# Attention in pairs of heads: 512-column value products, the output copied in the middle of a unit, and the adaLN sums moved by one unit

## The chip, the cores and the metric

The kernel is one program on one NeuronCore of a Trainium2 chip. The metric is the device time of one execution in microseconds. The kernel before takes 2616.31 us (median of 3 runs, 2615.91 to 2618.69).

Names used below: PE is TensorE (PEld its weight loads), DVE is VectorE, ACT is ScalarE, POOL is GpSimd, SP is the engine that issues most DMAs. "L988" is line 988 of the kernel before.

## What is computed

The reference is a two-layer encoder trunk on 1024 positions of width 1024, all in float32. Layer 0 mixes tokens by grouped-query softmax attention (16 query heads of 64, 4 key/value heads), layer 1 by a chunked gMLP; each is followed by a squared-ReLU MLP, and every sub-layer is modulated by vectors that come from the conditioning vector `c` (adaLN).

```python
for i in range(DEPTH):
    mod = cond @ ada_w[i] + ada_b[i]
    sh1, sc1, g1, sh2, sc2, g2 = jnp.split(mod, N_MOD, axis=-1)
    h = modulate(rmsnorm(x, norm1_g[i]), sh1, sc1)
    y = gqa_attention(...) if i % 2 == 0 else chunked_gmlp(...)
    x = x + g1[:, None, :] * y
    h = modulate(rmsnorm(x, norm2_g[i]), sh2, sc2)
    x = x + g2[:, None, :] * sq_relu_mlp(h, mlp_w_in[i], mlp_w_out[i])
...
def one_block(q_blk):
    s = jnp.einsum('bqkgd,bskd->bkgqs', q_blk, k).astype(jnp.float32) * scale
    p = jax.nn.softmax(s, axis=-1).astype(v.dtype)
    return jnp.einsum('bkgqs,bskd->bqkgd', p, v)
```

The change touches mostly the attention of layer 0.

## The kernel before

**Precision.** The fast matmul format of the kernel is fp32r. To keep float32 accuracy most operands are split into a rounded part `hi` (a copy on ACT, a CAST in the profile) and the rest `lo = x - hi` (a subtraction on DVE), and a product takes two or three matmuls: hi*hi, hi*lo, lo*hi.

**Attention, by units.** A unit is one head and a quarter of the queries: 256 queries, as two blocks of 128 (`j` = 0, 1). There are 64 units: 4 quarters (`qq`) by 4 key/value groups (`g`) by 4 heads (`h4`). Each unit goes through stages:

- s (L947, matmuls at L952): scores of one query block with all 1024 keys, 4 matmuls of 512 columns into a two-bank PSUM tile (`ps_s`, 2 tiles); then DVE takes the negated row maximum (L955).
- e (L958): ACT's exponential of the 1024 scores with the maximum as bias, row sums as a by-product (L961), from PSUM to an SBUF tile `p_`. It frees the score tile.
- t (L965): 4 PE transposes (L969) bring two 128-key chunks of both query blocks into one PSUM bank; ACT copies the bank to `hi` (L972).
- h (L975): DVE makes `lo` (L978), which frees the bank.
- v (L981): the value product. The values of a group lie as 128 stationary columns, 64 of their hi part and 64 of their lo part; a chunk of 128 keys is 2 matmuls (hi and lo of the probabilities) of 256 columns each (L988), 16 per unit, summed into `u.po`, half a PSUM bank. After the last, ACT copies the two 64-row halves of `po` out (L998, L1000).
- f (L1003): POOL adds the two halves (L1005), 64 x 256.

Transposed chunks and `po` share four PSUM banks (`p_x`, handed out by `bank_x`) with the query transposes (q) and small sums.

**The order is written out by hand.** `ORDER` lists the stages of one loop iteration; a letter, then the age of the unit it works on (0: this iteration's, 1: the one before, 2: two before), then the piece. `pin` keeps these instructions in this order on each engine's queue; instructions that are not pinned are placed by the scheduler when they are ready. An engine's queue runs in order, so an instruction that waits holds all behind it.

```python
ORDER = "s00 v20 t10 q10 h10 t11 e00 s01 h11 t12 h12 v21 t13 e01 h13 v22 v23 q00 f20 m00"
```

`q00` prepares queries on POOL every fourth iteration (`q_stage`, L679, unpinned), `q10` transposes them on PE and copies them on ACT in two of four (`q_trans`, L934). `m00` is the place for side work:

- iterations 2 to 13: squares, sums, reciprocal roots and rotary positions of the queries of the second half of the sequence (`late_sums`, `late_rope`, `late_rope1`);
- adaLN columns on DVE (`mod_ahead`, L218): a 512 KB load in every fourth iteration from 15 to 51, and in a later one a multiply with sum over 128x1024 (L225) and a 128x1 add (L226), ten times; in the kernel before this comes at the end of iterations i with i % 4 == 1;
- adaLN sums on POOL (`Slabs.step`, L186): a 128x1024 multiply (L197 or L199) and a 128x1024 add (L200), 24 steps from iteration 14 on, in iterations with i % 4 of 1 or 2 or i % 8 == 3;
- from iteration 53 on (`WO_AT`): normalising the finished first half for the output projection (`wo_sums`, `wo_prep`).

**Memory.** Tiles of 128x512 come from a pool "t" of 58 buffers (`slot`), of 128x1024 from small pools "w", "s" and "c". The probabilities `p_` lie in "c" (4 buffers). All later phases (the MLPs and gMLP, in Strassen-Winograd form with `split` forms of activations, and `Out`, the second products) share these pools.

Of the kernel before, what the change touches and what calls it, by code (L numbers as in the profile page):

```python
# [18 lines left out]
P = 128  # L19
# [17 lines left out]
def encoder_kernel(ctx: ExitStack, tc: tile.TileContext, t: dict, out: bass.AP):  # L37
# [22 lines left out]
    def slot(dt=F32, shape=(P, 512)):  # L60
        return mem.tile(list(shape), dt, tag="t", name=nm("t"), bufs=SLOTS["t"])

# [300 lines left out]
    def forms_b(f, xt, layer, which, rb, order, apart=False):  # L363
# [10 lines left out]
        def forms(kt):  # L374
# [8 lines left out]
            f[("6", kt)] = split(t2)  # L383
# [11 lines left out]
        def later(q):  # L395
            for kt in range(4):
                f[(q, kt)] = split(src[q][kt])
                src[q][kt] = None
# [149 lines left out]
    if True:  # L548
# [7 lines left out]
        def qkv_hi(cb, kp, keep):  # L556
            raw = wide("c", F32, (2, CB))
            nc.sync.dma_start(raw, t["wqkv"][cb, kp])
            for i in range(2):
                if not keep:  # L560
                    hi, lo = slot(F32R), slot(F32R)
# [78 lines left out]
        def qk_rope(src, i, tt, nt=1, eng=V, add=None):  # L640
# [4 lines left out]
            dst, t2 = slot(), slot()  # L645
            xv, tv = heads(src, nt), heads(t2, nt)
            hold(eng.tensor_tensor(heads(dst, nt), xv, tab(0, 0, HD), ALU.mult))
            for a, b in ((0, 32), (32, 0)):
                hold(eng.tensor_tensor(tv[:, :, :, a : a + 32], xv[:, :, :, b : b + 32], tab(1, a, 32), ALU.mult))
            hold((add or eng).tensor_tensor(dst, dst, t2, ALU.add))  # L650
            return dst

        def qk_rstd(ss):
            ms = ss.rearrange("p a b -> p (a b)")
            hold(V.tensor_scalar(ms, ms, 1.0 / HD, EPS, ALU.mult, ALU.add))
            return rsqrt_small(ms, ms.shape[1])

        def q_sums(src):
            return qk_rstd(qk_sums(src))
# [11 lines left out]
        def k_rows(hf, src):  # L671
            return [qk_rope(src[j], 1, hf * 4 + 2 * j, 2) for j in range(2)]
# [199 lines left out]
        qkv_mm(2, 1, ps, hs1)  # L872
# [33 lines left out]
    def wo_prep(hf, dt):  # L906
# [4 lines left out]
        hi, lo = slot(F32R), slot(F32R)  # L911
# [20 lines left out]
    with ExitStack() as es:  # L932
# [13 lines left out]

        def s_stage(u, j):  # L947
# [10 lines left out]
        def e_stage(u, j):  # L958
            ps, mx = u.s[j]
            p_ = wide("c")  # L960
            pin(S.activation(p_, ps, AF.Exp, bias=mx,  # L961
                             accum_out=rowsum[:, 2 * u.qq + j, u.head : u.head + 1]))
            u.p.append(p_)

        def t_stage(u, sp):  # L965
            pt = bank_x("t")
            for s in range(2):
                for j in range(2):
                    pin(T.transpose(pt[:, (2 * s + j) * P : (2 * s + j + 1) * P],  # L969
                                    u.p[j][:, (2 * sp + s) * P : (2 * sp + s + 1) * P], ident))  # L970
            hi = slot(F32R)
            pin(S.copy(hi, pt))  # L972
            u.t.append((pt, hi))

        def h_stage(u, sp):  # L975
            pt, hi = u.t[sp]
            lo = slot(F32R)
            pin(V.tensor_tensor(lo, pt, f32(hi), ALU.subtract))  # L978
            u.pt.append((hi, lo))

        def v_stage(u, sp):  # L981
            if sp == 0:
                u.po = bank_x("o", (P, 256))
            hi, lo = u.pt[sp]
            for s in range(2):
                st = 2 * sp + s
                for part, src in ((0, hi), (1, lo)):
                    pin(T.matmul(u.po, vt[st][:, u.g * P : (u.g + 1) * P], src[:, s * 256 : (s + 1) * 256],  # L988
                                 start=st == 0 and part == 0, stop=st == 7 and part == 1))
            if sp < 3:  # L990
                return
            dt, hf = u.head // 2, u.qq // 2
            if (dt, hf) not in ot:
                ot[(dt, hf)] = slot()
            a = (u.head % 2) * 64
            b = 64 - a
            dst = ot[(dt, hf)][a : a + 64, (u.qq % 2) * 256 : (u.qq % 2) * 256 + 256]
            pin(S.copy(dst, u.po[b : b + 64]))  # L998
            src = slot()[a : a + 64, :256]
            pin(S.copy(src, u.po[a : a + 64]))  # L1000
            u.fin = (dst, src)

        def f_stage(u, _):  # L1003
            dst, src = u.fin
            pin(G.tensor_tensor(dst, src, dst, ALU.add))  # L1005

        stages = dict(s=s_stage, e=e_stage, t=t_stage, h=h_stage, v=v_stage, f=f_stage)
        units = []
        for qq in range(4):
            for g in range(NKV):  # L1010
                for h4 in range(4):
                    u = Unit()
                    u.qq, u.g, u.h4, u.head = qq, g, h4, 4 * g + h4
                    u.s, u.p, u.t, u.pt = [], [], [], []
# [7 lines left out]
        qkv_mm(2, 2, ps, hs1)  # L1022
        units[0].qst = nxt
        s_stage(units[0], 0)
        e_stage(units[0], 0)
        qkv_mm(2, 3, ps, hs1, (0,))
        s_stage(units[0], 1)
        e_stage(units[0], 1)
        qkv_mm(2, 3, ps, hs1, (1,))
# [4 lines left out]
        def late_sums(j):  # L1034
            rr2[j] = q_sums(r2[j : j + 1])
# [16 lines left out]
        for i in range(nu + 2):  # L1052
            u0 = units[i] if i < nu else None
            u1 = units[i - 1] if 0 < i <= nu else None
            u2 = units[i - 2] if i > 1 else None
# [4 lines left out]
            for op in ORDER.split():  # L1060
                f, w, j = op[0], int(op[1]), int(op[2])
                if f == "m":
# [13 lines left out]
                    if late_mods and i % 4 == 1:  # L1076
# [9 lines left out]
                else:  # L1086
                    u = (u0, u1, u2)[w]
                    if u and (i or f not in "se"):
                        stages[f](u, j)
# [11 lines left out]
    class Out:  # L1101
# [73 lines left out]
        def split_f(self, k):  # L1175
            self.f[k] = split(self.raw.pop(k))
# [592 lines left out]
SLOTS = {"t": 58, "x": 16, "w": 4, "s": 5}  # L1769
# [100 lines left out]
```

## Time and profile before

| | us |
|---|---|
| median of 3 runs | 2616.31 |
| profiled execution | 2620.57 |
| its span, first to last instruction | 2618.8 |
| busy: PE / DVE / ACT / POOL | 2593.0 / 2179.8 / 1443.7 / 718.5 |
| attention units: first s to last v matmul begin | 153.0 to 548.5 |
| mean granted clock of PE | 0.998 |

The profile is of one execution. "Busy" of an engine is the time in which at least one of its instructions ran. PE's instructions overlap: a matmul's duration holds its latency, so what it costs in a stream is read from the distance between the starts of neighbours. The same holds, more weakly, of ACT and DVE: a CAST that is shown as 0.59 us lets the next begin after 0.48 us. In the views of instructions in time, a row is one instruction or a run of equal ones: its start, its length, engine, line, operation, tiles and count.

### The profile page before, as it was taken

To read this page: it belongs to the slowest core of one execution; us is meant where nothing else is said; L and a number is where in the kernel's file an instruction comes from. 1 tells how busy PE (TensorE), PEld (TensorE's weight loads), DVE (VectorE), ACT (ScalarE), POOL (GpSimd) and SP (SyncE) were. 2 spreads that over 40 slices of the span, in tenths; PEclk is the share of its full clock that TensorE was granted. 3 is DMA by queue.
4 is the path that set the end of the run, shared out by engine and by line. 5 is a ranking of instruction groups with operands and counts; after the bars stand their busy time and mean duration, and the time that the engine had idled before them with its cause. 6 is when DMAs were issued, how large, how long until landed. Compare 5 with 4: busy or idle time off the path is not lost.

```text
span 2618.8 us, 37177 instructions
## 1 busy us (share of the span) xinstructions
PE 2593.0 (99%) x12808; PEld 2167.8 (83%) x12808; DVE 2179.8 (83%) x3281; ACT 1443.7 (55%) x2584; POOL 718.5 (27%) x527
## 2 busy tenths in 40 slices
PE   9999999999999999999999999999999999999999
PEld 7889999887788888888888888888788788888887
DVE  7878999887989999877987687778889977789974
ACT  4579999845644555345543454445456644455442
POOL 0237876433000005430122055442420000005400
PEclk9999999999999999999999999999999999999999
DMA  8100222233586798544243454568641554497461
GB/s 289 45 1 9 89 82 76 89 130 128 195 284 242 279 310 301 181 137 169 81 153 113 137 175 169 174 216 298 228 142 52 182 176 159 148 313 264 150 212 58
DMA packets 209327, 434.33 MB, mean 166 GB/s; under 512 B 23089, under 2 KB 35505, under 8 KB 209138
## 3 DMA queue, kind: packets, MB, share of 16 engines
q1 hardware_dynamic: 182258, 394.19, 44.7%
q10 hardware_dynamic: 26880, 37.76, 4.0%
q8 instruction: 101, 1.65, 0.3%
q14 instruction: 88, 0.72, 0.1%
HBM read 309.18 MB, written 122.68 MB: 165 GB/s over the span
## 4 chain that ended last, share of the span: by engine, by line
PE 83%; DVE 9%; DMA 3%; ACT 3%; issue 1%; POOL 1%; SPq 0%; DVEq 0%; ACTq 0%; POOLq 0%
PE w L474 10%; PE w L475 10%; PE w L476 10%; PE out L1215 9%; PE out L1216 9%; PE out L1217 9%; PE s L952 4%; PE o L988 4%; PE t L969 4%; PE v L1574 3%; PE v L1573 3%; PE v L1572 3%; PE mix L1679 1%; DVE t L334 1%; DMA t<-hf 1%
## 5 line engine op out<-in xcount | busy, mean ns | idle before, releaser
L1215 PE MATMUL out<-t,s 128*128 128x512 f32 x1232 | 480.1, 390 | 2.5 <-ACT t L333 2.5
L1216 PE MATMUL out<-t,s 128*128 128x512 f32 x1232 | 480.0, 390 | 1.6 <-DVE t L334 1.6
L1217 PE MATMUL out<-t,s 128*128 128x512 f32 x1232 | 479.4, 390 | 0.0
L474 PE MATMUL w<-t,s 128*128 128x512 f32 x1168 | 458.5, 394 | 1.8 <-DVE c L1683 1.2
L475 PE MATMUL w<-t,s 128*128 128x512 f32 x1168 | 455.2, 390 | 1.8 <-DVE t L334 1.8
L476 PE MATMUL w<-t,s 128*128 128x512 f32 x1168 | 454.7, 389 | 0.0
L334 DVE TENSOR_TENSOR t<-t,t 128x512 fp32r<-128x512 f32 x408 | 323.8, 804 | 27.4 <-ACT t L333 20.2
L333 ACT CAST t<-t 128x512 fp32r<-128x512 f32 x408 | 244.8, 617 | 121.1 <-DMA t<-hf 71.3
L1215 PEld LDWEIGHTS out<-t,s 128*128 128x128 f32 x1232 | 231.6, 188 | 51.6 <-ACT t L333 3.7
L1216 PEld LDWEIGHTS out<-t,s 128*128 128x128 f32 x1232 | 231.7, 188 | 50.4 <-DVE t L334 2.9
L1217 PEld LDWEIGHTS out<-t,s 128*128 128x128 f32 x1232 | 231.7, 188 | 48.4
L459 ACT CAST s<-w 128x512 fp32r<-128x512 f32 x292 | 173.5, 616 | 161.8 <-PE w L476 104.7
L474 PEld LDWEIGHTS w<-t,s 128*128 128x128 f32 x1168 | 219.4, 188 | 49.6 <-issue 3.5
L475 PEld LDWEIGHTS w<-t,s 128*128 128x128 f32 x1168 | 219.4, 188 | 48.7 <-DVE t L334 5.2
L460 DVE TENSOR_TENSOR s<-w,s 128x512 fp32r<-128x512 f32 x292 | 221.8, 766 | 43.7 <-ACT s L459 43.0
L1197 ACT CAST s<-t 128x512 fp32r<-128x512 f32 x240 | 148.4, 621 | 197.2 <-PE out L1217 143.8
L476 PEld LDWEIGHTS w<-t,s 128*128 128x128 f32 x1168 | 219.3, 188 | 45.3
L1198 DVE TENSOR_TENSOR s<-t,s 128x512 fp32r<-128x512 f32 x240 | 195.7, 816 | 63.9 <-ACT s L1197 63.1
L1183 POOL TENSOR_TENSOR w<-w,t 128x512 f32<-128x512 f32 x20 | 33.5, 1684 | 765.7 <-DVE t L334 345.8
L955 DVE TENSOR_REDUCE mx<-s 128x1 f32<-128x1024 f32 x128 | 156.2, 1221 | 27.2 <-PE s L952 25.5
L978 DVE TENSOR_TENSOR t<-t,t 128x512 fp32r<-128x512 f32 x256 | 164.2, 682 | 17.3 <-ACT t L972 16.2
L988 PE MATMUL o<-t,t 128*128 128x256 f32 x1024 | 163.5, 292 | 0.0
(259 smaller groups left out, 5060.7 us busy)
## 6 DMA issues: line engine op xcount, KB each, us to landing
t<-hf SPq DMA_DIRECT2D x320, 256.0 KB, 4.0
hf<-c SPq DMA_DIRECT2D x156, 256.0 KB, 3.1
w<-in_wi_dram SPq DMA_DIRECT2D x64, 512.0 KB, 4.3
hf<-c ACTq DMA_DIRECT2D x96, 256.0 KB, 2.3
w<-in_ada_dram SPq DMA_DIRECT2D x36, 512.0 KB, 4.1
x<-in_ada_dram SPq DMA_DIRECT2D x64, 256.0 KB, 5.9
t<-in_wm_dram SPq DMA_DIRECT2D x64, 256.0 KB, 4.9
wf<-w SPq DMA_DIRECT2D x64, 256.0 KB, 2.9
```

The costliest lines, as they stand in the source:

```text
L333: S.copy(hi, src)
L334: (eng or V).tensor_tensor(lo, src, f32(hi), ALU.subtract)
L459: S.copy(hi, src)
L460: V.tensor_tensor(lo, src, f32(hi), ALU.subtract)
L474: T.matmul(ps, hi[:, a], th, start=kt == 0, stop=False)
L475: T.matmul(ps, hi[:, a], tl, start=False, stop=False)
L476: T.matmul(ps, lo[:, a], th, start=False, stop=kt == 3)
L988: pin(T.matmul(u.po, vt[st][:, u.g * P : (u.g + 1) * P], src[:, s * 256 : (s + 1) * 256], start=st == 0 and part == 0, stop=st == 7 and pa ...
L1198: V.tensor_tensor(lo, src, f32(hi), ALU.subtract)
L1215: T.matmul(ps, hi[:, a], th, start=begin and kt == 0, stop=False, **g)
L1216: T.matmul(ps, hi[:, a], tl, start=False, stop=False, **g)
L1217: T.matmul(ps, lo[:, a], th, start=False, stop=end and kt == 3, **g)
```

## The change

Two heads that share a key/value group form a pair of units (iteration n's and the next). Their four query blocks are transposed together, one 128-key chunk at a time, so that a chunk fills a bank with 4 x 128 queries and the value product of a chunk is 2 matmuls of 512 columns instead of 4 of 256. An even iteration transposes chunks 0 to 3 of the pair before and multiplies chunks 4 to 7 of the pair before that; an odd one transposes chunks 4 to 7 and multiplies chunks 0 to 3. The accumulated output, now a whole bank, is copied out by two 64x512 copies in the middle of each even iteration (`c20`); the two additions on POOL follow at its end. The loop runs one iteration longer at its end and starts at iteration 2, as units 0 and 1 are done among the last query projections. The adaLN columns on DVE come at the end of iterations with i % 4 == 0. One small operation of `late_sums` goes from DVE to POOL.

Around it: 16 of the 58 "t" buffers become 8 buffers "d" of 128x1024, which hold the probabilities, and later the hi/lo pairs of some splits; `norm_u` and `qk_rope` write in place; the first half's outputs lie in "c".

```diff
-        u = slot()
-        hold(V.scalar_tensor_tensor(u, xk, amod[:, layer, which, k : k + 1], rb, ALU.mult, ALU.mult))
-        return u
+        hold(V.scalar_tensor_tensor(xk, xk, amod[:, layer, which, k : k + 1], rb, ALU.mult, ALU.mult))
+        return xk
...
-    def split(src, eng=None):
-        hi, lo = slot(F32R), slot(F32R)
+    def split(src, eng=None, home=None):
+        hi, lo = home() if home else (slot(F32R), slot(F32R))
...
-        def qk_rstd(ss):
+        def qk_rstd(ss, eng=V):
             ms = ss.rearrange("p a b -> p (a b)")
-            hold(V.tensor_scalar(ms, ms, 1.0 / HD, EPS, ALU.mult, ALU.add))
+            hold(eng.tensor_scalar(ms, ms, 1.0 / HD, EPS, ALU.mult, ALU.add))
...
-        def t_stage(u, sp):
+        def t_stage(pr, c):
             pt = bank_x("t")
-            for s in range(2):
-                for j in range(2):
-                    pin(T.transpose(pt[:, (2 * s + j) * P : (2 * s + j + 1) * P],
-                                    u.p[j][:, (2 * sp + s) * P : (2 * sp + s + 1) * P], ident))
+            for n in range(4):
+                pin(T.transpose(pt[:, n * P : (n + 1) * P], pr.p[n][:, c * P : (c + 1) * P], ident))
...
+        def v_stage(pr, c):
+            if c == 0:
+                pr.po = bank_x("o")
+            for part, src in enumerate(pr.t[c]):
+                pin(T.matmul(pr.po, vt[c][:, pr.g * P : (pr.g + 1) * P], src,
+                             start=c == 0 and part == 0, stop=c == 7 and part == 1))
+
+        def c_stage(pr):
+            pr.src = [slot()[:64], slot()[:64]]
+            for i in range(2):
+                pin(S.copy(pr.src[i], pr.po[64 * i : 64 * i + 64]))
+
+        def f_stage(pr):
...
+            for i in range(2):
+                a, b = (r[:, i * 256 : (i + 1) * 256] for r in pr.src)
+                pin(G.tensor_tensor(dst[64 * i : 64 * i + 64, c0 : c0 + 256], a, b, ALU.add))
...
-        for i in range(nu + 2):
+        for i in range(2, nu + 3):
...
-            for op in ORDER.split():
+            for op in (EVEN, ODD)[odd].split():
...
-                    if late_mods and i % 4 == 1:
+                    if late_mods and i % 4 == 0:
                         late_mods.pop()()
...
-SLOTS = {"t": 58, "x": 16, "w": 4, "s": 5}
+SLOTS = {"t": 42, "x": 16, "w": 4, "s": 5, "d": 8}
...
-ORDER = "s00 v20 t10 q10 h10 t11 e00 s01 h11 t12 h12 v21 t13 e01 h13 v22 v23 q00 f20 m00"
+EVEN = "s00 v20 t10 h10 v21 q10 t11 e00 h11 v22 s01 v23 c20 t12 h12 t13 e01 h13 q00 f20 m00"
+ODD = "s00 t10 h10 v20 q10 t11 e00 v21 h11 s01 t12 h12 v22 t13 e01 h13 v23 q00 m00"
```

More of the change, by code (lines that the diff above doesn't have):

```diff
@@ L971, in t_stage, with h_stage @@
             hi = slot(F32R)
             pin(S.copy(hi, pt))
-            u.t.append((pt, hi))
-        def h_stage(u, sp):
-            pt, hi = u.t[sp]
+            pr.t[c] = (pt, hi)
+        def h_stage(pr, c):
+            pt, hi = pr.t[c]
             lo = slot(F32R)
             pin(V.tensor_tensor(lo, pt, f32(hi), ALU.subtract))
[L979 to L1008, printed above, removed]
+            pr.t[c] = (hi, lo)
+        def v_stage(pr, c):
[4 more added lines that the diff above has]
+                             start=c == 0 and part == 0, stop=c == 7 and part == 1))
@@ L1021, in encoder_kernel @@
         q_trans(qh, 1, nxt, bank_s)
[L1022 to L1029, printed above, removed]
+        qkv_mm(2, 1, ps, hs1, (1,))
+        for n, (kp, half) in enumerate(((2, 0), (2, 1), (3, 0), (3, 1))):
+            u = units[n // 2]
+            u.qst = nxt
+            s_stage(u, n % 2)
+            e_stage(u, n % 2)
+            qkv_mm(2, kp, ps, hs1, (half,))
+        qh = q_stage(units[4].qq, units[4].g)
+        cut(8)
         r2 = q_copies(ps)
```

76 lines of the change are left out of this document (51 added, 25 removed).

## The prediction

> **What bounds the kernel now.** I read the page's totals first, then the attention stage by windows, its chain of waits, and last each engine's instructions in time over one unit.
>
> ```profile
> span 2618.8 us, 37177 instructions
> ...
> PE 2593.0 (99%) x12808; PEld 2167.8 (83%) x12808; DVE 2179.8 (83%) x3281; ACT 1443.7 (55%) x2584; POOL 718.5 (27%) x527
> ```
>
> PE is busy all but 25.8 us of the span, so a change can gain only by giving PE less to do or by removing part of that idle time. The windows (length, busy time and count of PE, PEld, DVE, ACT, POOL, clock, DMA) show the attention stage:
>
> ```profile
> 300.00:350.00 50.00, 50.00 (x371) 46.42 (x370) 45.40 (x62) 44.69 (x91) 34.62 (x26) 1.00 0.23 75
> ```
>
> PE never stops, but DVE is busy for 45.40 of 50 us and ACT for 44.69: here, unlike in the 55% of the whole span, two more engines are close behind PE. The chain of waits over 240 to 260 us gives what a PE operation costs in the stream (start, share of the chain, line, count):
>
> ```profile
> 250.86 0.95 PE s L952 x4
> 251.80 0.44 PE t L969 x4
> 252.24 0.48 PE o L988 x4
> 252.72 0.44 PE t L969 x4
> 253.16 0.95 PE o L988 x8
> 254.11 0.93 PE s L952 x4
> ```
>
> So a 512-column matmul costs 0.2325 to 0.2375, a 256-column one 0.119 and a transpose 0.109. A unit is 2 x 0.94 + 4 x 0.44 + 16 x 0.119 = 5.54 us, and with a query transposition about 0.3 more.
>
> PE's waits between 160 and 545 us that matter (engine, line, released by: total, times, longest):
>
> ```profile
> PE t L969 <- DVE t L978: 3.4, 5, 1.0
> PE t L969 <- ACT c L961: 1.8, 3, 1.2
> ```
>
> That 5.2 us is nearly all that PE loses to others in the stage.
>
> **The change, part by part.** *Wide value products.* 16 x 0.119 = 1.904 us per unit become 8 x 0.2325 = 1.86: a 256-column matmul costs hardly more than half of a 512-column one. 64 units gain 2.8 us. With the 0.2375 of the other s group it is nothing; the other bound is a stretch of nothing but 512-column matmuls, 441 begun in 100 us or 0.227 each, which gives 5.6 us:
>
> ```profile
> 900.00:1000.00 100.00, 100.00 (x443) 82.84 (x442) 87.36 (x147) 57.97 (x105) 5.87 (x4) 1.00 0.90 312
> ```
>
> I take the 0.2325, as it stands between the same neighbours.
>
> *Output copied in the middle of an even unit.* Four 64x256 copies per pair become two of 64x512. Nearest rows: the 64x256 copy below (0.37) and this 128x512 one, which has the same columns:
>
> ```profile
> L1263 ACT COPY t<-out 128x512 f32<-128x512 f32 x24 | 14.1, 586 | 11.6 <-PE out L1217 11.5
> ```
>
> I take 0.59 each. ACT's total falls by about 0.3 us per pair, but all 1.2 us now stand in one unit, ahead of that unit's last two chunk copies. What that delays needs the queues. One unit before, on PE, ACT and DVE:
>
> ```profile
> 306.46 0.60 PE L969 MATMUL t<-ident,c 128*128 128x128 f32 x4
> 306.81 0.54 PE L938 MATMUL qt<-identr,t 128*128 128x128 f32 x4
> ```
>
> ```profile
> 306.39 0.37 ACT L1000 COPY t<-o 64x256 f32<-64x256 f32 x1
> 307.10 0.59 ACT L972 CAST t<-t 128x512 fp32r<-128x512 f32 x1 [0.33 <-PE t L969]
> 307.58 0.59 ACT L941 CAST t<-qt 128x512 fp32r<-128x512 f32 x1
> 308.06 0.60 ACT L972 CAST t<-t 128x512 fp32r<-128x512 f32 x1
> 308.93 1.12 ACT L961 ACTIVATE c<-s,mx 128x1024 f32<-128x1024 f32 x1 [0.27 <-DVE mx L955]
> 309.95 0.19 ACT L961 ACTIVATION_READ_ACCUMULATOR c<-s,mx 128x1 f32 x1
> 310.04 1.06 ACT L972 CAST t<-t 128x512 fp32r<-128x512 f32 x2
> ```
>
> ```profile
> 305.88 1.22 DVE L225 SCALAR_TENSOR_TENSOR w<-w,s 128x1024 f32<-128x1024 f32 x1
> 307.02 0.08 DVE L225 DVE_READ_ACCUMULATOR w<-w,s 128x1 f32 x1
> 307.14 0.57 DVE L226 TENSOR_TENSOR mod<-mod,cols 128x1 f32<-128x1 f32 x1
> 307.63 1.21 DVE L955 TENSOR_REDUCE mx<-s 128x1 f32<-128x1024 f32 x1
> 308.76 0.68 DVE L978 TENSOR_TENSOR t<-t,t 128x512 fp32r<-128x512 f32 x1
> 309.36 1.21 DVE L955 TENSOR_REDUCE mx<-s 128x1 f32<-128x1024 f32 x1
> ```
>
> From start to start: a chunk copy 0.48, an exponential 1.10, a maximum 1.13, a `lo` 0.60; PE to ACT takes 0.2 (four transposes from 306.46 end at 306.90, copy at 307.10); an exponential starts 0.09 after its maximum's end.
>
> Now an even iteration without query transposition, from its first s at 0. PE, by EVEN: v 0.94, t0 1.40, v 1.84, t1 2.30, v 2.73, s1 3.20, last v 4.13 to 4.60, t2 to 5.03, t3 to 5.47. ACT: copies t0 2.04, t1 2.93, exponential 3.41, the output copies 4.80 to 5.99, then t2 5.99, t3 6.47, exponential 6.95. DVE: `lo` of t2 6.60, of t3 7.20 to 7.80. The next (odd) unit's first s ends at 6.40 and its maximum could begin at 6.60, so DVE is 1.2 us late without any side work. In the odd unit PE asks for: t4 6.40, v (takes a bank for the new output) 6.84, t5 7.33, t6 9.16, t7 10.06. Four banks are shared, so t7 needs the `lo` of t4, which on DVE stands behind the maximum: 7.80 + 1.13 = 8.93, done at 9.61. In time, by 0.4. Where a query transposition takes a bank as well (i % 4 == 3), t5 waits for the even unit's last `lo`: about 0.27 by the same count, 16 times: **+4.3 us**.
>
> *adaLN column at i % 4 == 0.* It stands on DVE behind that late `lo`: 7.80 + 1.26 + 0.15 (the 128x1 add without a wait, the least of L158 under rival 1) = 9.21. Behind it are the odd unit's maximum (9.21), with it ACT's exponential (10.52) and all of ACT's later copies, and `lo` of t4 (10.34, done 11.02). PE's t7 now waits from 10.06 to 11.07: 1.0 us. The second maximum comes at 11.54, its exponential at 12.85 and ends with its accumulator at 14.06; the fourth transpose of the next even unit's t0 is due at 13.7 and waits another 0.4. In the kernel before the same work made the maximum 1.44 us late (307.63 against 305.99 + 0.2) and PE did not wait, because the second maximum stood ahead of the second `lo`. So 1.4 us for each of ten columns (iterations 16 to 52): **+14 us**. Bounds: 0, if the copies are short enough that DVE keeps within those 1.44 us, and 6 us each (rivals).
>
> *Side work at the start.* The sums of late queries (iterations 2, 4, 6, 8) wait on DVE for ACT's square as before, 5.6 us in four; what moves to POOL is the operation of the second row:
>
> ```profile
> L637 DVE TENSOR_REDUCE qss<-t 128x8 f32<-128x512 f32 x4 | 2.7, 686 | 5.6 <-ACT t L636 5.6
> ```
>
> ```profile
> L655 DVE TENSOR_SCALAR qss<-qss x9: 165/174/505, 99.4 to 210.3; 128x8 f32<-128x8 f32 x4, 128x32 f32<-128x32 f32 x3, 128x16 f32<-128x16 f32 x2
> ```
>
> It saves DVE 0.17 to 0.5 us four times, while a DVE that starts 1.2 late in odd units costs up to 1.4. Of the 3.4 us above I leave 3.4: 0, bounds -3.4 and +2.2. Units 0 and 1 among the projections: 12 matmuls of 0.23 cover each maximum and exponential; 0.
>
> *Loop end.* One more iteration, without s: the last pair's second half of transposes, copies and products stand one behind the other, with 24 output-projection matmuls (5.5 us) in between as cover. +1, bounds 0 and +2.
>
> *Buffers.* 16 + 42 "t" equivalents are as many as 58, but no longer exchangeable; writes in place change no count of instructions, and no DMA is moved past another. The work hidden behind PE's stream covers a later buffer: 0; with the cover gone a few waits of a copy each, -2 to +5 by the size of the idle time above.
>
> Sum: -2.8 + 4.3 + 14 + 0 + 1 + 0 = **+16.5 us**. The profiled execution took 2620.57 (1.8 beside the span), 4.3 over the median; on its own time that is 2637.1, on the median **2632.8**. Own range 2622 to 2641. A difference of 0.2%, 5.2 us, is about what a measurement of this kernel can tell from none.
>
> **Rivals.** *1. POOL holds DVE: 2659.* DVE's two-input operations wait for a running POOL addition to end:
>
> ```profile
> 563.65 2.41 POOL L117 TENSOR_TENSOR s<-w,s 128x1024 fp32r<-128x1024 f32 x1 [4.59 <-ACT s L116]
> ```
>
> ```profile
> 563.77 2.30 DVE L158 TENSOR_TENSOR mod<-mod,cols 128x1 f32<-128x1 f32 x1
> ```
>
> Both end at 566.07, though other such additions take this:
>
> ```profile
> L158 DVE TENSOR_TENSOR mod<-mod,cols x14: 149/160/2349, 543.0 to 596.2; 128x1 f32<-128x1 f32 x14
> ```
>
> The 0.57 of L226 above is the same, ended by the first of these:
>
> ```profile
> 306.90 0.78 POOL L1005 TENSOR_TENSOR t<-t,t 64x256 f32<-64x256 f32 x1 [4.87 <-ACT t L1000]
> 307.79 2.85 POOL L199 TENSOR_SCALAR w<-w,cols 128x1024 f32<-128x1024 f32 x1
> 310.72 2.40 POOL L200 TENSOR_TENSOR s<-s,w 128x1024 f32<-128x1024 f32 x1
> 313.08 0.73 POOL L1005 TENSOR_TENSOR t<-t,t 64x256 f32<-64x256 f32 x1
> ```
>
> POOL starts its next wide step as soon as the last addition is done, an iteration ahead of its place in the order. After the change, at i % 8 == 0: output copies end 5.99, additions 6.08 and 6.77, wide multiply 7.51; the column would start at 7.80, 0.3 too late. If the multiply holds DVE too: column 10.4 to 11.6, then the wide addition runs first, and the 128x1 add waits to 13.97. DVE comes back 4.8 us later than in my sum. Five times 4.8, and 0.6 in each of the other five (there POOL is behind and does short work): +27. For it: the margin. Against: no row shows a DVE wait on a TENSOR_SCALAR of POOL, and 0.3 us is about my error. The Trainium skill ("SBUF — State Buffer", Who interferes with whom) says that a DVE operation with two SBUF inputs and a GpSimd operation that reads SBUF exclude each other for the whole instruction; the trace agrees for additions (2.30 above), and by that rule this rival holds.
>
> *2. Nothing left: 2617.* The copies or DVE have 1.1 us more slack than I count, so that the column starts by 6.7 and fits; the bank waits of 4.3 eat the 2.8 of the wide products: +1.5. That the wide product isn't cheaper at all belongs here too: +4.
>
> *3. Faster: 2609.* Place: the t stages of the even units. All lo waits and the exponential's 1.2 go, as a product now follows its transposes by a whole unit and the first transpose of a chunk no longer needs the last exponential (its fourth does): -2.8 - 3.4 - 1.2 = -7.4. It decides from the point at which DVE is under 1.4 us late in odd units with a column in front. Against it: my 2.6.
>
> **How the numbers follow.** My forecast has 0.38, rival 1 0.22, rival 2 0.2, rival 3 0.2: the same count gives the rows of the unit before to 0.1 us (column 305.88, maximum 307.63), but the order after has no row. Slower 0.6, same 0.2 (rival 2), faster 0.2. The range 2609 to 2660 takes in the rivals' centres and leaves out a tenth at each end.
>
> **What would show it.** In the profile after: value matmuls 512 wide at 0.23 spacing, 512 of them; output copies of 0.59; DVE's `lo` as what PE's transposes wait for in odd units, some 1 us after each of ten L225-like columns and 0.27 at i % 4 == 3, some 18 us in all between 150 and 550 us. A 128x1 add of over 2 us beside a column means rival 1. No such waits and a stage of about 393 us would make the prediction wrong, as would a changed time of the phases behind 600 us.

## The result

The changed kernel takes 2636.98 us (median of 6 runs, 2633.93 to 2639.39) where the kernel before, run beside it, takes 2617.18 (2611.51 to 2623.01): ratio 1.0074, 95% interval 1.0060 to 1.0089. It is slower by some 19 us; 2632.8 was predicted. The profiled execution took 2635.8.

The page's span and busy time:

```profile
span 2634.0 us, 36190 instructions
...
PE 2596.4 (99%) x12296; PEld 2130.3 (81%) x12296; DVE 2177.6 (83%) x3277; ACT 1451.0 (55%) x2520; POOL 722.9 (27%) x531
```

PE now has 37.6 us without work (2634.0 - 2596.4), 11.8 more than before, with 512 matmuls fewer. The totals of DVE, ACT and POOL say nothing of where. The windows do: 50 us of attention without a drop of TensorE's granted clock, first of the kernel before, then of the changed one (columns as in the prediction):

```profile
260.00:310.00 50.00, 50.00 (x372) 46.30 (x371) 46.54 (x61) 46.26 (x93) 39.22 (x28) 1.00 0.26 85
```

```profile
260.00:310.00 50.00, 47.01 (x272) 37.52 (x272) 42.88 (x55) 41.64 (x76) 37.04 (x27) 1.00 0.22 74
```

PE loses 3 us in 50, and DVE and ACT are *less* busy than before. No engine has become the bound by its sum of work; the stage now loses time in a chain that goes from engine to engine. PE's waits from 150 to 570 us name its last link:

```profile
PE t L975 <- DVE t L983: 17.3, 14, 1.9
PE s L959 <- ACT d L968: 1.7, 4, 0.9
```

17.3 us in 14 waits for DVE's subtraction `lo`, against 3.4 in 5 before. Ten of the 14 follow the ten adaLN columns. One of them on PE, in time (in brackets the wait before it):

```profile
311.46 0.66 PE L975 MATMUL t<-ident,d 128*128 128x128 f32 x4 [1.53 <-DVE t L983]
```

The chain that ended last, from 300 to 326 us, shows how it comes about (start, us, engine, tile, line):

```profile
304.37 0.59 ACT t L996
...
304.97 0.58 ACT t L996
...
305.58 0.60 ACT t L977
...
306.20 1.29 DVE t L983 x2
307.49 2.00 DVE w L229 x2
...
309.51 0.16 DVE mod L230
309.67 1.14 DVE mx L962
310.81 1.19 DVE t L983 x2
312.00 1.14 DVE mx L962
...
313.17 1.22 ACT d L968 x2
...
314.43 0.33 PE t L975
```

Read it from the top: two output copies of 0.59 and 0.58 hold ACT, so the copy of the last transposes but one comes late; DVE's two subtractions come 1.2 us late with it; then the column holds DVE for 2.00 us; behind it stand the next unit's maximum, two subtractions, the second maximum and ACT's exponential; and PE's transpose at 314.43 has waited for that exponential. The transposes at 311.46 waited for the bank that the subtractions at 310.81 free. For ten us nothing of this chain is PE's: PE works beside it until it runs out of released work. The links are those that the prediction counted.

The predicted signs are there too: 512 value products of 512 columns and 64 output copies of 0.58 us:

```profile
L990 PE MATMUL o<-t,t x512: 387/397/775, 171.5 to 575.6; 128*128 128x512 f32 x171
```

```profile
L996 ACT COPY t<-o x64: 579/583/590, 181.3 to 576.7; 64x512 f32<-64x512 f32 x64
```

By stretches, from the starts of the first score, last value product and first `w` matmul (L477; before, L474) in each trace, in us; "no columns" and the two kernels behind it are experiments 1, 8 and 4 below:

| | before, and again | after | no columns | units before, no columns | before with the new buffers, and again |
|---|---|---|---|---|---|
| to the first score | 153.2, 152.0 | 155.1 | 152.6 | 155.2 | 152.2, 156.2 |
| first score to last value product | 395.3, 394.8 | 420.5 | 399.4 | 395.4 | 397.0, 395.1 |
| from there to the first `w` | 86.7, 87.1 | 87.0 | 87.0 | 86.7 | 86.9, 86.7 |
| the rest | 1983.6, 1982.2 | 1971.4 | 1971.5 | 1975.0 | 1977.3, 1975.1 |

So attention lost 25 us, and the phases behind it gave 11 to 12 back. The first row varies by 4 us between executions of one kernel and says nothing. The second row holds stretches in which TensorE was granted half its clock: 6.8 us in the changed kernel, 3.4 us in both traces of the kernel before, in "no columns" and in the first of the new buffers, none in the other two. Counting half of each as lost (an estimate for a stage that PE bounds), attention takes 393.5 and 393.2, 417.1, 397.6, 395.4, and 395.3 and 395.1 us.

### The profile page after: what moved, and what is told of

It reads as the page before. It is cut to its first block, busy times and chain, and to the rows that moved or that the text cites. A ratio compares the mean times of both kernels' runs of the same rounds, so it can differ in the third digit from the quotient of the medians.

```text
span 2634.0 us, 36190 instructions
## 1 busy us (share of the span) xinstructions
PE 2596.4 (99%) x12296; PEld 2130.3 (81%) x12296; DVE 2177.6 (83%) x3277; ACT 1451.0 (55%) x2520; POOL 722.9 (27%) x531
## 4 chain that ended last, share of the span: by engine, by line
PE 84%; DVE 9%; ACT 4%; issue 1%; DMA 1%; POOL 0%; SPq 0%; ACTq 0%; DVEq 0%
PE out L1231 11%; PE out L1232 11%; PE out L1230 11%; PE w L477 10%; PE w L478 10%; PE w L479 10%; PE o L990 3%; PE v L1588 3%; PE v L1589 3%; PE v L1587 3%; PE s L959 3%; PE t L975 2%; PE mix L1694 2%; DVE t L983 2%; DVE mx L962 1%
## 5 line engine op out<-in xcount | busy, mean ns | idle before, releaser
L1230 PE MATMUL out<-d,s 128*128 128x512 f32 x1232 | 479.6, 389 | 0.0
L1232 PE MATMUL out<-d,s 128*128 128x512 f32 x1232 | 479.3, 389 | 0.0
L1231 PE MATMUL out<-d,s 128*128 128x512 f32 x1232 | 479.3, 389 | 0.0
L477 PE MATMUL w<-t,s 128*128 128x512 f32 x816 | 321.4, 394 | 0.0
L478 PE MATMUL w<-t,s 128*128 128x512 f32 x816 | 318.4, 390 | 1.6 <-DVE t L337 1.5
L479 PE MATMUL w<-t,s 128*128 128x512 f32 x816 | 317.7, 389 | 0.0
L337 DVE TENSOR_TENSOR d<-t,d 128x512 fp32r<-128x512 f32 x332 | 270.9, 836 | 3.4 <-ACT d L336 2.9
L1230 PEld LDWEIGHTS out<-d,s 128*128 128x128 f32 x1232 | 231.3, 188 | 48.3
L1231 PEld LDWEIGHTS out<-d,s 128*128 128x128 f32 x1232 | 231.3, 188 | 47.9
L1232 PEld LDWEIGHTS out<-d,s 128*128 128x128 f32 x1232 | 231.3, 188 | 47.7
L1213 DVE TENSOR_TENSOR s<-t,s 128x512 fp32r<-128x512 f32 x240 | 187.5, 783 | 66.2 <-ACT s L1212 66.1
L336 ACT CAST d<-t 128x512 fp32r<-128x512 f32 x332 | 203.0, 620 | 28.5 <-DMA t<-hf 16.0
L983 DVE TENSOR_TENSOR t<-t,t 128x512 fp32r<-128x512 f32 x256 | 169.2, 686 | 53.1 <-ACT t L977 51.7
L478 PEld LDWEIGHTS w<-t,s 128*128 128x128 f32 x816 | 153.3, 188 | 34.5 <-DVE t L337 4.1
L477 PEld LDWEIGHTS w<-t,s 128*128 128x128 f32 x816 | 153.3, 188 | 32.5 <-issue 1.4
L479 PEld LDWEIGHTS w<-t,s 128*128 128x128 f32 x816 | 153.2, 188 | 31.7
L990 PE MATMUL o<-t,t 128*128 128x512 f32 x512 | 176.9, 428 | 0.0
L975 PE MATMUL t<-ident,d 128*128 128x128 f32 x1024 | 154.8, 277 | 20.5 <-DVE t L983 17.3
```

The source lines that it names most:

```text
L477: T.matmul(ps, hi[:, a], th, start=kt == 0, stop=False)
L478: T.matmul(ps, hi[:, a], tl, start=False, stop=False)
L479: T.matmul(ps, lo[:, a], th, start=False, stop=kt == 3)
L975: pin(T.transpose(pt[:, n * P : (n + 1) * P], pr.p[n][:, c * P : (c + 1) * P], ident))
L990: pin(T.matmul(pr.po, vt[c][:, pr.g * P : (pr.g + 1) * P], src, start=c == 0 and part == 0, stop=c == 7 and part == 1))
L1230: T.matmul(ps, hi[:, a], th, start=begin and kt == 0, stop=False, **g)
```

## The experiments

The theory going in: a column at i % 4 == 0 stands on DVE behind subtractions that the output copies make late, and pushes the next unit's maxima and exponentials past the point where PE needs them. The rivals: POOL's wide multiply holds the column to its end (rival 1); the pairs themselves are dearer; a column costs its DVE time wherever it stands. Ratios are to the kernel before, run on the same chip.

| | median, us | ratio, 95% interval |
|---|---|---|
| changed kernel | 2636.98 | 1.0074 [1.0060, 1.0089] |
| 1 no columns | 2613.0 | 0.9984 [0.9975, 0.9994] |
| 2 columns at i % 4 == 3 | 2617.92 | 1.0003 [0.9993, 1.0013] |
| 3 columns at i % 4 == 1 | 2621.22 | 1.0024 [1.0015, 1.0034] |
| 4 before, new buffers | 2613.7 | 0.9987 [0.9978, 0.9997] |
| 4 again | 2614.99 | 0.9991 [0.9982, 1.0000] |
| 5 output copies later | 2629.51 | 1.0052 [1.0037, 1.0067] |
| 6 column in the gap | 2623.69 | 1.0030 [1.0020, 1.0039] |
| 7 no wide sums on POOL | 2628.57 | 1.0047 [1.0031, 1.0062] |
| 8 units before, no columns | 2612.38 | 0.9989 [0.9979, 0.9998] |
| 9 column before the scores | 2614.45 | 0.9993 [0.9984, 1.0001] |
| 10 halved products | 2615.13 | 0.9999 [0.9990, 1.0008] |

**1. The columns left out.**

Their loads go too, and the sums they form are a constant.

```diff
-                    if late_mods and i % 4 == 0:
-                        late_mods.pop()()
                     if i % 4 == 3 and 12 <= i < 52:
-                        late_mods.append(mod_ahead())
+                        pending.pop(0)
```

> The kernel after with the ten adaLN columns on DVE (loads, 128x1024 multiply-sums and 128x1 adds) left out; those modulation values are then a constant. Theory A (a column behind DVE's late lo holds up the odd unit's maximum): the ten PE waits of 1.3 to 2.0 us in odd units and the ten of 0.29 that follow them go, groups of four units fall from about 25.0 to about 23.1 us, the whole by 19 us to about 2618. Theory B (the order by pairs is short of banks whatever DVE does): the waits stay at over half their size and the whole falls by under 8 us.

2613.0 us, where theory A had 2618; theory B is excluded. The ten columns cost 0.0090 of 2617, some 23.5 us, more than all that the change lost. (It is the columns and not their loads: experiment 9, below, has both and takes 2614.45.) Without them the pairs are 0.16% *under* the kernel before. To see the price of one, take the start of the first exponential in units 20 and 24. Without columns, then with them:

```profile
273.59 1.13 ACT L970 ACTIVATE d<-s,mx 128x1024 f32<-128x1024 f32 x1
...
296.70 1.12 ACT L970 ACTIVATE d<-s,mx 128x1024 f32<-128x1024 f32 x1
```

```profile
278.19 1.12 ACT L968 ACTIVATE d<-s,mx 128x1024 f32<-128x1024 f32 x1
...
303.07 1.12 ACT L968 ACTIVATE d<-s,mx 128x1024 f32<-128x1024 f32 x1
```

Four units take 23.11 us without and 24.88 with a column: 1.8 us. (Over units 16 to 51, leaving out the four in which the clock dropped, the mean is 1.9.)

**2 and 3. The columns in odd units**, each a change of one number in the condition (`== 3`, `== 1`).

> The kernel after with the columns at the end of iterations i % 4 == 3 instead of 0. Theory A: behind an odd unit there are no output copies ahead of lo, so DVE is less late and most of the waits go: 10 to 14 us less than after, about 2624. Theory B (a column costs its own length on a DVE that is full, wherever it stands): no change, 2637 within 4. If POOL's running multiply is what counts (theory C), 4 us less, as five of the columns start beside one.

> The kernel after with the columns at the end of iterations i % 4 == 1, where the kernel before has them. Theory A: also behind an odd unit, but POOL's wide addition runs there and holds a two-input DVE operation to its end: 4 to 8 us less than after, about 2631, and columns or 128x1 adds of 1.5 to 2.5 us in the profile. Theory B: no change. If the place among POOL's sums does not matter, the same as with i % 4 == 3.

2617.92 and 2621.22: the place decides, as expected, but both are faster than theory A's 2624 and 2631; theories B and C, at 2633 and more, are excluded. In units i % 4 == 3 a column costs 0.5 us (4.9 us over experiment 1), in units i % 4 == 1 0.8. PE's waits for `lo` fall from 17.3 us to 5.0 and 6.1.

**5. The output copies behind the last copy of the unit**, the columns where the change put them. It takes the first two links out of the chain above and puts the two copies ahead of the unit's second exponential.

```diff
-EVEN = "... s01 v23 c20 t12 h12 t13 e01 h13 q00 f20 m00"
+EVEN = "... s01 v23 t12 h12 t13 c20 e01 h13 q00 f20 m00"
```

> The changed kernel with one entry of the even order moved: the two output copies stand behind the copy of the last transposes (t13) instead of ahead of the copy of t12; everything else, the ten columns too, is as in the changed kernel (2636.98 us). Theory P (the column is dear because of where it lies: the chain in the trace runs output copy 0.59, output copy 0.58, copy of t12 0.60, subtraction 1.29 for two, column 2.00, sum 0.16, maximum, exponential; so what holds the column back is ScalarE, 1.2 us late by the two output copies): the column starts earlier, and a count of the two queues with the durations of the trace gives some 8 us less, 2629 us, with PE's waits for the subtraction (L983) down from 17.3 us to under 11. Rival V (a column costs its 2 us of VectorE wherever ScalarE's copies lie): no change, 2634 to 2640 us.

2629.51. The waits of the transposes for `lo` fell:

```profile
PE t L975 <- DVE t L983: 5.2, 9, 0.9
```

The chain in the same pair as above:

```profile
302.32 0.60 ACT t L977
302.94 1.29 DVE t L983 x2
304.23 1.15 DVE w L229 x2
305.41 0.56 DVE mod L230
305.97 1.13 DVE mx L962
```

The output copies are no longer in it, and this column ends its 1.15 us unhindered. Of the 23.5 us only some 6 are regained (0.0022 in ratio, with an uncertainty of about as much). The traces say where the rest went. In units 16 to 51, without the four in which the changed kernel's clock dropped, four units take 24.41 us on average against 25.31 in the changed kernel and 23.39 without columns: half of a column's 1.9 is gone. But units 12 to 15, which have no column, take 23.48 against 23.10: the copies now stand ahead of the exponential, and the new order by itself costs 0.4. So the link of the output copies is shown; part of the delay has changed engines.

**6. The column in the gap behind the output copies**: same unit, some 5 us earlier, where DVE waits for ACT anyway.

```diff
-EVEN = "... v23 c20 t12 h12 t13 e01 h13 q00 f20 m00"
+EVEN = "... v23 c20 l00 t12 h12 t13 e01 h13 q00 f20 m00"
+                elif f == "l":
+                    if late_mods and i % 4 == 0:
+                        late_mods.pop()()
```

> The changed kernel with the ten columns in the same units (i%4 == 0) but issued some 5 us earlier on VectorE: between the second maximum and the subtraction for t12, where VectorE waits for ScalarE's two output copies (1.18 us) and the copy of t12 in any case. Work, buffers and transfers are unchanged. Theory P (place inside the unit): most of a column goes into that wait; the count of the queues gives 11 us less, 2626 us, and PE's waits for the subtraction (L983) under 9 us instead of 17.3. Rival V (the column's VectorE time is paid in any even unit, only the odd units have slack): 2634 to 2640 us. The column two units on (i%4 == 3) gave 2617.9, so a value as low as that would mean that the unit does not matter at all, only what stands next to it.

2623.69, 0.0044 or 11.5 us under the changed kernel with the same work in the same unit, as counted (11): rival V falls. PE's waits for `lo` did not fall as far as expected, to 11.6 us and not 9.

**7. No wide sums on POOL.** It asks what POOL has to do with it. In the changed kernel POOL and DVE meet like this at 305 to 310 us:

```profile
305.63 1.54 POOL L1005 TENSOR_TENSOR c<-t,t 64x256 f32<-64x256 f32 x2 [2.58 <-ACT t L996]
307.28 2.85 POOL L203 TENSOR_SCALAR w<-w,cols 128x1024 f32<-128x1024 f32 x1
```

```profile
307.41 2.06 DVE L229 SCALAR_TENSOR_TENSOR w<-w,s 128x1024 f32<-128x1024 f32 x1
309.40 0.08 DVE L229 DVE_READ_ACCUMULATOR w<-w,s 128x1 f32 x1
309.51 0.16 DVE L230 TENSOR_TENSOR mod<-mod,cols 128x1 f32<-128x1 f32 x1
```

POOL's multiply starts 0.13 us ahead of the column, the order that rival 1 needs. The column takes 2.06 us instead of 1.22, but it is done at 309.40, while the multiply runs to 310.13; and the 128x1 addition, with two SBUF inputs as well, takes 0.16 beside it. All ten:

```profile
L229 DVE SCALAR_TENSOR_TENSOR w<-w,s x10: 1215/1687/2062, 257.3 to 489.6; 128x1024 f32<-128x1024 f32 x10
```

```profile
L230 DVE TENSOR_TENSOR mod<-mod,cols x10: 159/364/953, 259.4 to 490.9; 128x1 f32<-128x1 f32 x10
```

The edit, which leaves the adaLN product out of three groups:

```diff
-            if dt == 0:
-                self.acc[g] = wide("s")
-                pin(G.tensor_scalar(self.acc[g], raw, condc[:, 0:1], None, ALU.mult))
-            else:
-                pin(G.tensor_scalar(raw, raw, condc[:, dt : dt + 1], None, ALU.mult))
-                pin(G.tensor_tensor(self.acc[g], self.acc[g], raw, ALU.add))
             if dt == KT - 1:
+                self.acc[g] = raw
```

> The changed kernel with GpSimd's wide adaLN sums left out (the multiplications and additions of 128x1024 in attention; the loads and the small matmuls stay, on the last loaded part, so three adaLN groups are not what the reference has). The columns stand where they stand. Theory H (a GpSimd multiplication of one 128x1024 input holds a column for about 0.85 us of its 2.85): five columns 0.85 us each, some 4 us less, up to 8 by the count of the queues since the other VectorE work is freer too: 2629 to 2633 us. Rival 1 of the prediction (a column waits out GpSimd's whole multiplication, 4.8 us at five columns): some 24 us less, 2613 us. Rival N (GpSimd is nowhere in the path): 2635 to 2639 us.

2628.57, 0.0027 or some 7 us under the changed kernel. Every column now takes 1.22 us and every addition 0.16. By the rows of the changed kernel POOL's hold is five times 0.85 at the columns, and at the additions four times 0.41 (0.57 for 0.16) and once 0.79 (0.95): 6.7 us. The gain measured, 7 us with an uncertainty of some 6, agrees with that and with theory H's 4 to 8, whose 4 had left out the additions; the attention of the two traces differs by 6 (417.1, with half of the low clock left out, against 411.1). Rival 1's 24 us and rival N's nothing are excluded. The other 13 to 14 of the ten columns' 19 to 20 us in the traces (411.1 against 397.6) remain without POOL.

**4 and 8. What is not columns.** Experiment 4 is the kernel before with the new buffers alone (`SLOTS`, the writes in place, the splits in pairs, the probabilities in "d", the first half's outputs in "c"); experiment 8 is that without columns and their loads, so that against experiment 1 only the units differ.

> The kernel before with the buffers of the change alone: 42 + 8 wide, probabilities and split pairs in the wide ones, norm and rotary positions in place, first outputs in the other pool; units, order and columns as before. Theory D (the 12 us that the change gives back behind the attention come from the buffers): the phases behind 660 us lose 12 us as in the kernel after, the attention stays within 3 us: about 2606. Theory E (they come from the attention's other end, which leaves the adaLN values and loads earlier or later): no change, 2617 within 4.

> The kernel before with the new buffers (2613.7 us) and without the ten columns: their loads and products are left out and the sums they form are constants, as in the changed kernel without columns (2613.0 us). Against that kernel it differs by the units alone: single heads with 256-column value products instead of pairs with 512-column ones. By the terms of the prediction (wide products -2.8, bank waits at i%4 == 3 +4.3, loop end +1, start 0) the pairs cost 2.5 us, so 2610.5 us here; the columns of the kernel before would then cost 3 us. Rival W (the pairs are worth their 2.8 us or more, and the bank waits are hidden): 2614 to 2617 us. Rival Z: the pairs cost the whole of what attention showed beyond the columns, some 4 to 6 us: 2607 to 2609 us.

> The kernel before with the new buffers alone, once more, for a closer ratio and a second trace of the phases behind attention. Before: 0.9987 [0.9978, 0.9997]; expected 0.998 to 0.999, some 2612 to 2615 us. Theory K (what the phases behind attention wait for belongs to the kernel): again some 5 us of waits for a split's source or a late transfer, which the kernels with pairs do not have, and 1976 to 1978 us from the first matmul of wo's weight phase to the end. Rival N (they are chance, from one execution to the next): 1971 to 1974 us this time.

> The kernel before itself, for a second trace. Theory K: the phases behind attention take 1983 us again, with some 5 us of PE waiting for the split copies (L333). Rival N: those waits are chance: 1972 to 1980 us, other waits.

Experiment 4 gave 0.9987 and 0.9991, 2.4 to 3.4 us by ratio: within the 4 us of theory E, far from theory D's 2606. Experiment 8 gave 2612.38 us and 0.9989, between the 2610.5 expected and rival W's 2614: the pairs of experiment 1 are 1.3 us faster by ratio, with intervals that include no difference; and the kernel before pays nothing measurable for its columns (0.9987 and 0.9991 with, 0.9989 without). In attention the traces are finer. By the starts of the same exponentials as above, four units take 22.76 us in experiment 8 (276.15 and 298.91) and 23.11 in experiment 1: the pairs cost 0.35 in four units.

The bank wait that the prediction counted at i % 4 == 3 is in the trace of experiment 1. On PE, the query transposes (qt) and the transposes behind them, in units 22 (i % 4 == 2) and 23; below them DVE's `lo` in unit 23:

```profile
283.44 0.46 PE L944 MATMUL qt<-identr,t 128*128 128x128 f32 x4
283.74 0.62 PE L977 MATMUL t<-ident,d 128*128 128x128 f32 x4
...
288.93 0.53 PE L944 MATMUL qt<-identr,t 128*128 128x128 f32 x4
289.52 0.66 PE L977 MATMUL t<-ident,d 128*128 128x128 f32 x4
```

```profile
288.18 1.29 DVE L985 TENSOR_TENSOR t<-t,t 128x512 fp32r<-128x512 f32 x2 [1.15 <-ACT t L979]
```

In unit 22 the transposes begin 0.30 us after the query transposes, in unit 23 0.59, just behind the end of the two `lo` (289.47). It is so in each of the 12 units i % 4 == 3 from 7 to 51, by 0.30 us: 3.6 us. The view of waits does not list them: the query transposes are shown as running until 289.46, so PE's idle time there is only 0.06.

Behind attention the buffers show. PE's waits from 630 to 2600 us in the kernel before:

```profile
PE out L1215 <- ACT t L333: 2.5, 3, 2.0
PE w L474 <- ACT t L333: 2.1, 2, 1.6
PE w L475 <- DVE t L334: 1.8, 6, 0.5
...
PE w L474 <- DVE c L1683: 1.2, 1, 1.2
```

and, its largest, in experiment 4 again and in the changed kernel:

```profile
PE w L477 <- DVE c L1688: 2.4, 3, 1.4
PE w L478 <- DVE t L337: 1.6, 4, 0.8
```

```profile
PE w L478 <- DVE t L337: 1.5, 4, 0.8
```

The waits for the split copies (L333), 5.1 us with a smaller one at `v`, are gone with the new buffers. The second trace of the kernel before has them again (4.7 us) and 1982.2 us behind attention, so they belong to it, not to chance; experiment 4 repeated its 1977.3 with 1975.1, experiment 8 has 1975.0. The kernels with pairs have 1971.3 to 1973.6. All waits of PE in this view add up to 11.2 us in the kernel before, to 8.9 and 7.1 in experiment 4, 7.4 in experiment 8 and 4.2 in the changed kernel. So waits account for most of the differences, and the wait for `c` is the largest that the units before keep. Why it goes with the pairs, in phases whose instructions stand in the same order as in experiment 4, is not settled.

In attention the new buffers cost something: with half of the low clock left out it takes 395.1 to 395.4 us in the three traces that have them, with the units before, and 393.2 to 393.5 in the two of the kernel before. That is why the times show less than the phases behind give.

**10. Each wide product made as two halves**, in the kernel of experiment 1 (no columns).

```diff
-                pin(T.matmul(pr.po, vt[c][:, pr.g * P : (pr.g + 1) * P], src,
...
+                for b in range(2):
+                    pin(T.matmul(pr.po[:, b * 256 : (b + 1) * 256], vt[c][:, pr.g * P : (pr.g + 1) * P],
+                                 src[:, b * 256 : (b + 1) * 256],
```

> The changed kernel without columns (2613.0 us), and each 512-column value product made as two of 256 columns side by side in the same bank; columns of adaLN are left out and the value sums are not those of the reference in the two halves' order. It prices the wide product by itself. The prediction's term is 2.8 us for 64 units (0.119 against 0.2325 a matmul); by the spacing that the changed kernel's trace shows (0.235) it is 1.5: 2614.5 to 2616 us. Rival F (an extra weight load for each matmul is not hidden): 512 more loads of some 0.1 us would be far above, 2640 us or more. Rival Z: no difference, 2613 us.

2615.13 against 2613.0, 0.0015 in ratio (3.9 us), at the edge of what can be told. In the trace four units (starts 276.67 and 299.93) take 23.26 against 23.11: 0.15, or 2.4 us for 64 units; the mean over units 16 to 51 is 0.11, or 1.8 us. The 512 additional weight loads cost no more than this: PEld's busy time rises from 2128.9 to 2166.8 us, and nearly all of it lies beside matmuls.

**9. The columns ahead of the second scores**, the best place by the count.

```diff
-EVEN = "... h11 v22 s01 v23 c20 ..."
+EVEN = "... h11 v22 l00 s01 v23 c20 ..."
+                    if late_mods and i % 4 == 2:
+                        late_mods.pop()()
```

> All the work of the reference, in pairs of heads as in the changed kernel, with the ten columns issued in the even units i%4 == 2 just ahead of the second scores, some 6 us earlier in the unit than the gap behind the output copies. VectorE has nothing ready there but the subtraction of t11 before and the second maximum behind it, and the maximum waits for PE's scores. Theory P (what counts is how late VectorE and ScalarE stand at that point of the order): the count of the queues gives 17 us less than the changed kernel, within 1 us of no columns at all: 2614 to 2619 us, no more than 1.5 us of waits for the subtraction behind any column. Rival V2 (a column ahead of a maximum delays the exponential behind it, and the transposes behind that, by 1 to 1.4 us, ten times): 2624 to 2628 us.

2614.45, 0.0081 or 21 us under the changed kernel with the same ten columns; rival V2's 2624 is excluded. It is 1.5 us (2.4 by ratio) over no columns at all, less than can be told: in units 16 to 51 the nine columns cost 0.2 us together, and behind attention this trace has 1973.1 us against 1971.5. A column there is (DVE, in time):

```profile
307.99 0.69 DVE L983 TENSOR_TENSOR t<-t,t 128x512 fp32r<-128x512 f32 x1 [0.69 <-ACT t L977]
308.60 1.22 DVE L229 SCALAR_TENSOR_TENSOR w<-w,s 128x1024 f32<-128x1024 f32 x1
309.74 0.08 DVE L229 DVE_READ_ACCUMULATOR w<-w,s 128x1 f32 x1
309.86 0.16 DVE L230 TENSOR_TENSOR mod<-mod,cols 128x1 f32<-128x1 f32 x1
309.94 1.22 DVE L962 TENSOR_REDUCE mx<-s 128x1 f32<-128x1024 f32 x1
```

No POOL operation holds it (1.22 and 0.16), DVE was waiting for ACT before it, and the maximum behind it is early enough. Against the kernel before, its ratio of 0.9993 [0.9984, 1.0001] is no difference that can be told; the smallest ratio with all the work done is experiment 4's, by about 0.1%. No version here beats the kernel before by the 0.2% of the prediction.

## Why the prediction came out as it did

The mechanism, its place and the sign were right. The sum, +16.5, was 3 us short of the 19.4 that the ratio gives. That is closer than its terms were, and so in part luck: a column term that was too small stood beside a gain behind attention that was put at nothing. So is the total of PE's waits for `lo`, 17.3 us where some 18 were counted: 14.7 of it follow the columns, where the count had 10, and the bank waits are not in it.

- *adaLN column, +14.* Mis-sized: 23.5 us by the times of experiment 1. In the trace it is 21.1 in attention (420.5 - 399.4), of which a longer drop of the clock is some 1 to 2, so 19 to 20. The runs of the changed kernel have a mean granted clock of 0.9975 and those of experiment 1 of 0.9988; for a kernel that PE bounds that is an estimated 3.4 us, so the rest of the 23.5 may be the clock. Per four units the column cost 1.9 where the prediction counted 1.4. The step that failed is "7.80 + 1.26 + 0.15": column and addition take what they take without POOL. With POOL's wide sums gone, the same four-unit distances exceed those of experiment 1 by 1.2, close to the counted 1.4, and POOL's hold is the other 0.7. The links themselves (output copies, late subtractions, maximum, exponential, fourth transpose) stand in the chain as counted.
- *Wide products, -2.8.* 1.8 to 2.4 in the trace of experiment 10; confirmed within 1 us.
- *Bank waits, +4.3, and loop end, +1.* The bank waits are in the trace where they were counted, 0.30 us twelve times (3.6) for 0.27 sixteen times. The loop end was not tried alone. With the wide products the two made +2.5; experiment 1 against 8 shows 4.0 over all of attention (399.4 - 395.4), about 1.7 of it a drop of the clock in experiment 1 (3.4 us at half clock, taken as half lost). The net term was right.
- *Start, 0.* Not resolved: the start varies by 4 us from execution to execution.
- *Buffers, 0, bounds -2 to +5.* Wrong: some 5 to 9 us less behind attention in the traces of experiments 4 and 8, outside the bounds (up to 1.7 of it a drop of the clock in the first trace of the kernel before, at 1870 us) and some 2 more in attention, which leaves the 2.4 to 3.4 of the times. The step that failed is "the work hidden behind PE's stream covers a later buffer": it asked only whether a buffer would come later, not whether the kernel before already waited for one. Its 5.1 us for split copies behind 600 us could be read in the same view of waits that was read for attention only. The prediction named a changed time of those phases as a sign of being wrong, and this term was; with the unsettled rest of 1 to 6 us it offset the column's excess.
- *Rival 1.* Its condition was met: POOL's multiply came first in five of ten columns, by 0.13 us where 0.3 was counted. Its price was not: 0.85 us a column, not the rest of 2.85. By the Trainium skill ("SBUF — State Buffer", Who interferes with whom) the two exclude each other for the whole instruction; this case's trace differs for a multiplication with one SBUF input (the column ran to its end 0.7 us before the multiply did, as far as the profile's rough spans on POOL go), and the measurement decides. For POOL's two-input additions the rows agree with the rule: the 128x1 additions of 0.57 us end with one.
- *Rivals 2 and 3.* At this place of the column DVE had neither the slack of rival 2 nor the lead of rival 3. Rival 2's 2617 is what the units i % 4 == 3 give (2617.92). Rival 3's 2609 was not reached even without columns (2613.0).

## What to carry to other kernels

Side work on an engine that is not the bound is priced by what stands behind it in that engine's queue and by when the bound engine wants that, not by its length: the same ten columns of 1.4 us cost nothing measurable in the kernel before and at their best place in the pairs, and some 20 us at their worst. Before placing it, list for each slot how late the engine already is there and which copy on the neighbouring engine made it late; a gap of waiting on that engine is the place to look for. And read the waits of the stages that an edit touches only by its buffers too: a wait that is there already is what a buffer can remove.

## What the hardware showed

A POOL multiply of 128x1024 with one SBUF input (2.85 us) that began 0.13 us ahead of a DVE operation with two SBUF inputs delayed it by 0.85 us and no more, five times of five, and a second such operation ran in 0.16 us beside it. The other way about, a column that began together with it (332.67 us) ran its 1.22 us, the 128x1 addition behind it took 0.95, and the multiply 3.93:

```profile
332.67 3.93 POOL L203 TENSOR_SCALAR w<-w,cols 128x1024 f32<-128x1024 f32 x1
```

Both orders are what a multiply would show that keeps such a DVE operation out for its first 0.8 to 1.0 us only (an estimate from these rows); other lengths were not tried.

The granted clock dropped in the middle of attention of the profiled execution after (windows, the clock is third from the end):

```profile
338.00:340.00 2.00, 2.00 (x15) 2.00 (x15) 1.70 (x4) 1.42 (x3) 1.06 (x1) 0.74 0.00 0
340.00:342.00 2.00, 2.00 (x6) 1.52 (x6) 0.43 (x2) 0.00 (x0) 0.00 (x0) 0.50 0.72 262
...
344.00:346.00 2.00, 2.00 (x11) 1.85 (x10) 0.69 (x1) 0.98 (x3) 0.00 (x0) 0.55 0.00 0
```

It is 6.8 us at half clock, from 339 to 345.8 us; the four units there took 29.75 us, some 3 more than the 24.92 of the same four without columns and 1.9 for a column. Such a drop adds a few us to one execution; whether longer waits of PE bring it about was not tried.
